# Batched x·y on one core: loading each block of x two batches earlier and splitting its transposes into halves

## The chip, the cores and the metric

One core of one Trainium2 chip. The metric is device time in microseconds (us), the median of the runs given. All runs quoted are fast (on one core: within 1.5% of the fastest of the same kernel) unless the text says otherwise. A profiled run has a span about 1.8 us shorter than its device time (134.7 us against 136.52 for the kernel before), because the span counts from the program's first instruction to its last.

In the profile PE is the matrix engine (PEld its weight loads); ACT, DVE and POOL work on elements; SP issues the transfers, and SPq is its queue. HBM is the memory outside the core, SBUF the core's own, and PSUM the one that PE writes its results to. The granted clock is the share of PE's full speed that the throttle allowed. A DMA share adds up the recorded times of all packets and divides by sixteen engines' time; it can exceed 1, so the records must overlap a little.

## The reference

```python
batch, dim_i, dim_j, dim_k = 32, 256, 512, 384     # x: b,i,j   y: b,j,k   float32
def reference(x, y):
    return np.einsum('bij,bjk->bik', x, y).astype(np.float32)
```

That is 32 independent products of 256 x 512 by 512 x 384. x is 16.8 MB, y 25.2 MB and the result 12.6 MB, so 54.5 MB cross between HBM and SBUF.

## The kernel before

x is loaded in blocks of Q = 4 batches (2048 KB in one transfer), y batch by batch (768 KB), and results are stored batch by batch (384 KB). The products need x transposed. PE does that in 32 transposes per block into PSUM; ACT and DVE copy the transposed tiles out as fp16 ("evictions", eight of 128x512 per block). ACT and DVE also round y to fp16 and copy the products out of PSUM ("collect"). All transfers are issued from one queue, SP, in program order.

```python
def load(b):
    if b % Q == 0:                       # x of batches b..b+3, just before y of b
        x_of[b // Q] = x_pool.tile([P, R, J], F32, name="x_sb")
        keep(nc.sync.dma_start(out=x_of[b // Q], in_=x[b : b + Q]...))
    y_of[b] = y_pool.tile([P, NJ, K], F32, name="y_sb")
    keep(nc.sync.dma_start(out=y_of[b], in_=y[b]...))

def transpose(q):                        # a whole block: 4 x 2 tiles
    for t in range(NJ):
        for e in range(NI):
            ...                          # 4 PE transposes into t_ps
            if n % 2 == 0: keep(nc.vector.tensor_copy(dst, t_ps))
            else:          keep(nc.scalar.copy(dst, t_ps))
# ... cut: round_y, multiply, collect, store ...

ahead = LAG - 2                          # LAG = 8: loads run six batches ahead
for b in range(ahead): load(b)
for s in range(B + 2):
    if s + ahead < B:          load(s + ahead)
    if s >= 2:                 collect(s - 2)
    if 1 <= s <= B:            multiply(s - 1)
    if s < B and s % Q == 0:   transpose(s // Q)
    if s < B:                  round_y(s)
    if s >= 2:                 store(s - 2)
```

Buffers that matter: 3 of x, 10 of y, 2 of transposed x, 10 of results, 4 PSUM banks for transposes and 4 for products.

Of the kernel before, what the change touches and what calls it, by code (L numbers as in the profile page):

```python
# [1 line left out]

# [5 lines left out]


MM_DT = mybir.dt.float16  # L10
F32 = mybir.dt.float32
P = 128


Q = 4

LAG = 8

ON_ACT = ()


@with_exitstack
def kernel(
    ctx: ExitStack,
    tc: tile.TileContext,
    x: bass.AP,
    y: bass.AP,
    out: bass.AP,
):
    nc = tc.nc  # L30

    B, I, J = x.shape
    _, _, K = y.shape

    NI = I // P
    NJ = J // P


    R = Q * NI
    PQ = P // Q  # L40

    const_pool = ctx.enter_context(tc.tile_pool(name="const", bufs=1))
    x_pool = ctx.enter_context(tc.tile_pool(name="x_pool", bufs=3))
    y_pool = ctx.enter_context(tc.tile_pool(name="y_pool", bufs=10))
    yr_pool = ctx.enter_context(tc.tile_pool(name="yr_pool", bufs=4))
    xt_pool = ctx.enter_context(tc.tile_pool(name="xt_pool", bufs=2))
    o_pool = ctx.enter_context(tc.tile_pool(name="o_pool", bufs=10))
    tpsum_pool = ctx.enter_context(tc.tile_pool(name="tpsum", bufs=4, space=bass.MemoryType.PSUM))
    opsum_pool = ctx.enter_context(tc.tile_pool(name="opsum", bufs=4, space=bass.MemoryType.PSUM))


    keep = tc.keep_in_program_order

    identity = const_pool.tile([P, P], F32)
    make_identity(nc, identity)

    x_of, y_of, yr_of, xt_of, ps_of, o_of = {}, {}, {}, {}, {}, {}

    def load(b):
        if b % Q == 0:  # L60
            x_of[b // Q] = x_pool.tile([P, R, J], F32, name="x_sb")
            keep(
                nc.sync.dma_start(  # L63
                    out=x_of[b // Q],
                    in_=x[b : b + Q].rearrange("g (p r) j -> (g p) r j", r=R),
                )
            )
        y_of[b] = y_pool.tile([P, NJ, K], F32, name="y_sb")
        keep(nc.sync.dma_start(out=y_of[b], in_=y[b].rearrange("(q t) k -> q t k", q=P)))  # L69

    def transpose(q):




        x_sb = x_of.pop(q)
        xt_of[q] = xt_pool.tile([P, Q, NJ, NI, PQ, Q], MM_DT, name="xt_sb")
        n = 0
        for t in range(NJ):
            for e in range(NI):  # L80
                t_ps = tpsum_pool.tile([P, Q, Q, PQ], F32, name="t_ps")
                for h in range(Q):
                    keep(
                        nc.tensor.transpose(  # L84
                            t_ps[:, h].rearrange("c g p -> c (g p)"),
                            x_sb[:, h * NI + e, t::NJ],
                            identity,
                        )
                    )
                dst = xt_of[q][:, :, t, e].rearrange("c g p h -> c h g p")  # L90
                if n % 2 == 0:
                    keep(nc.vector.tensor_copy(dst, t_ps))  # L92
                else:
                    keep(nc.scalar.copy(dst, t_ps))  # L94
                n += 1

    def round_y(b):
        y_sb = y_of.pop(b)
        yr_of[b] = yr_pool.tile([P, NJ, K], MM_DT, name="y_r")
        for t in range(NJ):  # L100
            if t % 2 == 0:
                keep(nc.scalar.copy(yr_of[b][:, t], y_sb[:, t]))  # L102
            else:
                keep(nc.vector.tensor_copy(yr_of[b][:, t], y_sb[:, t]))  # L104

    def multiply(b):
        xt_sb, y_r = xt_of[b // Q][:, b % Q], yr_of.pop(b)
        ps_of[b] = [
            opsum_pool.tile([P, K], F32, name=f"o_ps_{e}", tag="o_ps")
            for e in range(NI)  # L110
        ]
        for t in range(NJ):
            for e in range(NI):
                keep(
                    nc.tensor.matmul(  # L115
                        ps_of[b][e],
                        xt_sb[:, t, e].rearrange("c p h -> c (p h)"),
                        y_r[:, t],
                        start=(t == 0),
                        stop=(t == NJ - 1),  # L120
                    )
                )

    def collect(b):
        o_of[b] = o_pool.tile([P, NI, K], F32, name="o_sb")
        for e in range(NI):
            if e % 2 == 0:
                keep(nc.scalar.copy(o_of[b][:, e], ps_of[b][e]))  # L128
            else:
                keep(nc.vector.tensor_copy(o_of[b][:, e], ps_of[b][e]))  # L130
        del ps_of[b]

    def store(b):
        eng = nc.scalar if b in ON_ACT else nc.sync
        keep(eng.dma_start(out=out[b].rearrange("(m e) k -> m e k", m=P), in_=o_of.pop(b)))


    ahead = LAG - 2
    for b in range(ahead):
        load(b)  # L140
    for s in range(B + 2):
        if s + ahead < B:
            load(s + ahead)
        if s >= 2:
            collect(s - 2)
        if 1 <= s <= B:
            multiply(s - 1)
        if s < B and s % Q == 0:
            transpose(s // Q)
        if s < B:  # L150
            round_y(s)
        if s >= 2:
            store(s - 2)


# [1 line left out]
_INS = ['x', 'y']  # L157
_OUTS = [((32, 256, 384), 'float32')]


# [23 lines left out]
```

## Time and profile before

| | before |
|---|---|
| device time, median of 3 (range) | 136.25 us (136.09 to 136.34) |
| span of the profiled run | 134.7 us |
| busy PE / ACT / DVE | 89.5 / 80.1 / 73.7 us |
| 16 DMA engines busy with data | 97.9% of the span |
| mean rate over the span | 405 GB/s |

How to read it: start with the rows that can be full. No compute engine is; the DMA engines are. Then ask whether an average hides a stage with another limit. One view is who made the compute engines wait; the columns are total us, number of waits, longest.

```profile
ACT xt_sb L94 <- PE t_ps L84: 43.9, 16, 8.7
DVE xt_sb L92 <- PE t_ps L84: 40.2, 18, 9.8
...
PE t_ps L84 <- DMA x_sb<-in_x_dram: 24.3, 7, 8.7
```

These are the waits that the change is aimed at. ACT and DVE stood for some 40 us each in front of an eviction. Laid over PE's own waits, ACT's 43.9 us are 22.3 us in which PE stood before a transpose whose x had not landed (6.7 of them at the start) and 21.6 us in which PE was at work; DVE's 40.2 us are 24.3 and 15.9.

### The profile page before, as it was taken

To read this page: it belongs to the slowest core of one execution; us is meant where nothing else is said; L and a number is where in the kernel's file an instruction comes from. 1 tells how busy PE (TensorE), PEld (TensorE's weight loads), DVE (VectorE), ACT (ScalarE), POOL (GpSimd) and SP (SyncE) were. 2 spreads that over 40 slices of the span, in tenths; PEclk is the share of its full clock that TensorE was granted. 3 is DMA by queue.
4 is the path that set the end of the run, shared out by engine and by line. 5 is a ranking of instruction groups with operands and counts; after the bars stand their busy time and mean duration, and the time that the engine had idled before them with its cause. 6 is when DMAs were issued, how large, how long until landed. Compare 5 with 4: busy or idle time off the path is not lost.

```text
span 134.7 us, 1539 instructions
## 1 busy us (share of the span) xinstructions
PE 89.5 (66%) x512; PEld 66.6 (49%) x512; DVE 73.7 (55%) x128; ACT 80.1 (59%) x129; POOL 0.7 (1%) x6
## 2 busy tenths in 40 slices
PE   0049499769677908949794983949459492794920
PEld 0048368644564408925492543936259360793510
DVE  0008855975397503873489340796228870378720
ACT  3007994996299602795479650699218990179910
POOL 2000000000000000000000000000000000000000
PEclk9999999999999985686999599599995999559995
DMA  5999999999999999999999999999999999999992
GB/s 131 399 413 423 447 412 416 416 434 414 404 422 451 425 399 424 421 435 437 400 416 430 438 425 410 421 418 454 407 409 425 433 440 402 421 421 413 412 410 84
DMA packets 10375, 54.62 MB, mean 405 GB/s; under 512 B 1152, under 2 KB 1152, under 8 KB 9344
## 3 DMA queue, kind: packets, MB, share of 16 engines
q1 hardware_dynamic: 10368, 54.53, 97.9%
q8 instruction: 4, 0.07, 0.2%
q14 instruction: 3, 0.02, 0.0%
HBM read 41.94 MB, written 12.58 MB: 405 GB/s over the span
## 4 chain that ended last, share of the span: by engine, by line
DMA 79%; PE 8%; ACT 5%; DVE 2%; issue 2%; SPq 1%; DVEq 0%
DMA y_sb<-in_y_dram 30%; DMA x_sb<-in_x_dram 27%; DMA out_dram<-o_sb 21%; PE o_ps L115 4%; PE t_ps L84 4%; ACT xt_sb L94 2%; ACT y_r L102 2%; DVE xt_sb L92 1%; DVE y_r L104 1%; DVE o_sb L130 0%; SPq L69 0%; ACT o_sb L128 0%; SPq L63 0%; DVEq L130 0%
## 5 line engine op out<-in xcount | busy, mean ns | idle before, releaser
L94 ACT CAST xt_sb<-t_ps 128x512 f16<-128x512 f32 x32 | 39.8, 1350 | 44.0 <-PE t_ps L84 43.9
L92 DVE CAST xt_sb<-t_ps 128x512 f16<-128x512 f32 x32 | 40.1, 1323 | 40.3 <-PE t_ps L84 40.2
L84 PE MATMUL t_ps<-identity,x_sb 128*128 128x128 f32 x256 | 43.4, 340 | 24.5 <-DMA x_sb<-in_x_dram 24.3
L115 PE MATMUL o_ps<-y_r,xt_sb 128*128 128x384 f16 x256 | 46.3, 342 | 14.9 <-ACT y_r L102 14.9
L84 PEld LDWEIGHTS t_ps<-identity,x_sb 128*128 128x128 f32 x256 | 41.1, 216 | 27.8 <-issue 26.4
L115 PEld LDWEIGHTS <-xt_sb 128*128 128x128 f16 x256 | 26.2, 102 | 34.2 <-issue 19.9
L102 ACT CAST y_r<-y_sb 128x384 f16<-128x384 f32 x64 | 30.2, 527 | 0.6 <-DMA y_sb<-in_y_dram 0.6
L130 DVE COPY o_sb<-o_ps 128x384 f32<-128x384 f32 x32 | 17.8, 556 | 15.1 <-PE o_ps L115 15.1
L104 DVE CAST y_r<-y_sb 128x384 f16<-128x384 f32 x64 | 19.9, 354 | 0.4 <-DMA y_sb<-in_y_dram 0.4
L128 ACT COPY o_sb<-o_ps 128x384 f32<-128x384 f32 x32 | 15.4, 483 | 3.8 <-PE o_ps L115 3.8
L94 ACT ACT_TABLE_LOAD x1 | 1.3, 1283 | 0.7 <-PEq L168 0.7
masks.py:199 POOL TENSOR_SCALAR_AFFINE_SELECT identity<-identity 128x128 f32<-128x128 f32 x1 | 0.3, 294 | 0.1
masks.py:197 POOL MEMSET identity<- 128x128 f32 x1 | 0.2, 205 | 0.3 <-POOLq L168 0.3
L168 POOL MEMSET const-bfloat16-1.0<- 128x1 bf16 x1 | 0.1, 102 | 0.0
L168 POOL MEMSET const-uint8-127<- 128x1 uint8 x1 | 0.1, 102 | 0.0
L168 POOL MEMSET const-float32-0.0<- 128x1 f32 x1 | 0.1, 99 | 0.2 <-issue 0.2
L168 POOL MEMSET const-float32-1.0<- 128x1 f32 x1 | 0.1, 99 | 0.0
## 6 DMA issues: line engine op xcount, KB each, us to landing
y_sb<-in_y_dram SPq DMA_DIRECT2D x32, 768.0 KB, 15.1
x_sb<-in_x_dram SPq DMA_DIRECT2D x8, 2048.0 KB, 14.2
out_dram<-o_sb SPq DMA_DIRECT2D x32, 384.0 KB, 14.1
```

What stands on the lines that cost most here:

```text
L84: nc.tensor.transpose(t_ps[:, h].rearrange("c g p -> c (g p)"), x_sb[:, h * NI + e, t::NJ], identity,)
L92: keep(nc.vector.tensor_copy(dst, t_ps))
L94: keep(nc.scalar.copy(dst, t_ps))
L102: keep(nc.scalar.copy(yr_of[b][:, t], y_sb[:, t]))
L104: keep(nc.vector.tensor_copy(yr_of[b][:, t], y_sb[:, t]))
L115: nc.tensor.matmul(ps_of[b][e], xt_sb[:, t, e].rearrange("c p h -> c (p h)"), y_r[:, t], start=(t == 0), stop=(t == NJ - 1),)
L128: keep(nc.scalar.copy(o_of[b][:, e], ps_of[b][e]))
L130: keep(nc.vector.tensor_copy(o_of[b][:, e], ps_of[b][e]))
L168: nc = _bacc.Bacc("TRN2", target_bir_lowering=False, num_devices=1)
```

## The change

The intent: each block of x is loaded two batches earlier, and its 32 transposes no longer stand as one block between the products of two batches. They follow the products of the two preceding steps in halves of 16, so that products, stores and transposes mix.

```diff
+    def load_x(q): ...                  # the same transfer as before
     def load(b):
-        if b % Q == 0: ...              # x block of b
+        if b == 0:
+            load_x(0)
+        if b % Q == Q - 2 and b + 2 < B:
+            load_x((b + 2) // Q)
         ...
-    def transpose(q):
+    def transpose(q, half):
-        for t in range(NJ):
+        for t in range(half * NJ // 2, (half + 1) * NJ // 2):
 ...
+        if s == 0:
+            transpose(0, 0)
+            transpose(0, 1)
         if s >= 2:
             collect(s - 2)
         if 1 <= s <= B:
             multiply(s - 1)
-        if s < B and s % Q == 0:
-            transpose(s // Q)
         if s < B:
             round_y(s)
+        for half in range(2):
+            if s % Q == Q - 2 + half and s + 2 < B:
+                transpose(s // Q + 1, half)
```

More of the change, by code (lines that the diff above doesn't have):

```diff
@@ L57, with load_x @@
     x_of, y_of, yr_of, xt_of, ps_of, o_of = {}, {}, {}, {}, {}, {}
-    def load(b):
-        if b % Q == 0:
-            x_of[b // Q] = x_pool.tile([P, R, J], F32, name="x_sb")
-            keep(
-                nc.sync.dma_start(
-                    out=x_of[b // Q],
-                    in_=x[b : b + Q].rearrange("g (p r) j -> (g p) r j", r=R),
-                )
-            )
+    def load_x(q):
+        x_of[q] = x_pool.tile([P, R, J], F32, name="x_sb")
+        keep(
+            nc.sync.dma_start(
+                out=x_of[q],
+                in_=x[q * Q : (q + 1) * Q].rearrange("g (p r) j -> (g p) r j", r=R),
+            )
+        )
+    def load(b):
+        if b == 0:
+            load_x(0)
+        if b % Q == Q - 2 and b + 2 < B:
+            load_x((b + 2) // Q)
         y_of[b] = y_pool.tile([P, NJ, K], F32, name="y_sb")
         keep(nc.sync.dma_start(out=y_of[b], in_=y[b].rearrange("(q t) k -> q t k", q=P)))
-    def transpose(q):
-        x_sb = x_of.pop(q)
-        xt_of[q] = xt_pool.tile([P, Q, NJ, NI, PQ, Q], MM_DT, name="xt_sb")
+    def transpose(q, half):
+        x_sb = x_of[q]
+        if half == 0:
+            xt_of[q] = xt_pool.tile([P, Q, NJ, NI, PQ, Q], MM_DT, name="xt_sb")
         n = 0
-        for t in range(NJ):
+        for t in range(half * NJ // 2, (half + 1) * NJ // 2):
             for e in range(NI):
```

## The prediction

> **What bounds the kernel now.** I read the page first: busy shares, the 40 slices, the DMA queue line.
>
> ```profile
> PE 89.5 (66%) x512; PEld 66.6 (49%) x512; DVE 73.7 (55%) x128; ACT 80.1 (59%) x129; POOL 0.7 (1%) x6
> ...
> DMA  5999999999999999999999999999999999999992
> ...
> q1 hardware_dynamic: 10368, 54.53, 97.9%
> ...
> HBM read 41.94 MB, written 12.58 MB: 405 GB/s over the span
> ```
>
> No compute engine is above 66%, while the one data queue fills 97.9% of sixteen DMA engines' span, and every slice but the first and the last is full. The kernel is a copy with arithmetic beside it.
>
> Then the chain of waits, to see whether that average hides a stage with another limit.
>
> ```profile
> DMA 79%; PE 8%; ACT 5%; DVE 2%; issue 2%; SPq 1%; DVEq 0%
> ```
>
> The 8% of PE and 5% of ACT could be taken for the price of the transposes. So I asked for DMA share and rate by stage (columns: stretch, length, busy time of the engines, granted clock, DMA share, GB/s).
>
> ```profile
> 3.00:18.65 15.65, 7.87 (x46) 6.69 (x47) 6.78 (x10) 7.43 (x11) 0.00 (x0) 1.00 1.00 421
> 18.65:110.30 91.65, 68.00 (x395) 49.65 (x394) 56.19 (x101) 60.22 (x101) 0.00 (x0) 0.89 1.02 423
> 110.30:123.00 12.70, 8.31 (x43) 7.27 (x42) 6.21 (x8) 5.68 (x7) 0.00 (x0) 0.73 0.99 412
> 123.00:131.00 8.00, 5.36 (x32) 3.03 (x31) 4.53 (x12) 5.50 (x14) 0.00 (x0) 1.00 1.02 412
> ```
>
> The share stays at 0.99 to 1.02 in the loads before the first store, in the steady part, in the stretch with the last block of transposes (PE's clock down to 0.73), and in the stores at the end. The rate moves by 3%. No stage has another limit.
>
> Last, the waits of the queue that issues every transfer, and the end of its timeline.
>
> ```profile
> SPq L135 <- DMA x_sb<-in_x_dram: 28.7, 6, 6.0
> SPq L135 <- DMA y_sb<-in_y_dram: 26.6, 18, 1.5
> SPq L69 <- DMA out_dram<-o_sb: 11.3, 20, 0.6
> SPq L135 <- DVE o_sb L130: 11.2, 6, 4.0
> ```
>
> ```profile
> 110.31 0.33 SPq L69 DMA_DIRECT2D y_sb<-in_y_dram  x1
> 115.23 14.73 SPq L135 DMA_DIRECT2D out_dram<-o_sb  x9
> ```
>
> A store at L135 doesn't read x, yet it waits for an x transfer. Numbering the 72 transfers in order of issue, from the ninth on each leaves only when the one eight places before it has landed: y6 at 8.58 us, when x0 had landed at 8.56; y7 at 10.44 after y0 at 10.43; x2 at 12.34 after y1 at 12.32. So eight are in flight, and a wait for a transfer means that the queue is full. The fourth line is another thing: six stores waited 11.2 us in all for compute, 4.0 us at most, with seven transfers under way (store 23, at 115.23, is the start of the last nine).
>
> **What the Trainium skill says.** "DMA: Bandwidth & Descriptors", section "Where 436 GB/s comes from", puts the ceiling of the sixteen SBUF ports at 435 GB/s and a measured 16 MB load at 425. The trace agrees: 421 to 423 while the queue is full, so there is no rate to win. The same page, section "Why a DMA increments its semaphore by 16 and not by 1", says that up to sixteen engines work on one transfer and finish independently, and that only the full count means landed. The trace's landing records show it: the ten transfers that landed first (28.5 us and before) had 0.8 us between their first and last engine; all later ones have 2.1 to 2.5 us. "TensorE: Matmul & The Clock Gate", section "What's actually happening", says that an idle PE drops to half clock. The trace shows grants of 0.5 after each long wait for x. The change may help here, but PE doesn't set the end.
>
> **The change part by part.**
>
> 1. Loads of x moved ahead by two batches. Removed: nothing; added: nothing. It stays 8 x loads of 2048 KB, 32 y loads of 768 KB and 32 stores of 384 KB. From the packet records one engine's share is 64 packets of 16 KB at 0.611 us, 256 of 6 KB at 0.234 and 256 of 3 KB at 0.121: 39.1 + 59.9 + 31.0 = 130.0 us. The slowest engine began at 1.74 and ended at 133.58, 131.84 us. The other 1.8 us are slow first packets (1.0 to 2.1 us each) and one 16 KB instruction fetch of 1.1 us at 28.4, beside which an x packet took 1.08 instead of 0.61. The slowest engine has thus no idle time to give back. Effect: 0.
>
> 2. Transposes in two halves. Still 256 transposes and 64 evictions of the same shapes. A half is 16 transposes (32 took 4.54 us at full clock, so 2.3) and two evictions on each of ACT and DVE, 2 x 1.35 = 2.7 us. On ACT a step with a half costs 2.7, plus two roundings 2 x 0.527 and a collection 0.483: 4.2 us; a step without one 1.5. Batches arrive every (768 + 384) KB at 421 GB/s, 2.8 us, and a block of x takes 5.0 us more: 4 x 2.8 + 5.0 = 16.2 us per four batches, against 16.1 between the x issues at 52.83 and 68.89. ACT needs 2 x 4.2 + 2 x 1.5 = 11.4 of those. Two steps with halves fall 2 x 1.4 = 2.8 us behind, and the next two win 2.6 back, before the pause of 5.0 for the next x. PE waits for x (24.3 us over 7 in the groups of instructions) should shrink or move to waits for y. This is all beside the DMA.
>
> 3. Could stores become late enough to hurt? A transfer takes 14.1 (stores) to 15.1 us (y) from issue to landing at the median, nearly all of it queueing. A store held for 4 us leaves over 9 us of queued work; a delay of 2.8 us does so all the more. Effect in the middle: 0.
>
> 4. The start. After the change x1 goes before y2, so y2 lands at about 14.2 + 5.0 = 19.2 us rather than 14.20. Batch 0's store left at 18.65 and can leave only when the transfer eight before it, now y2, has landed, 0.5 us later, with seven loads queued. Effect: 0.
>
> 5. The end. y31's load is issued after store 22 and before store 23 in both programs, so the same transfers stand before it and the same nine stores after it. On the slowest engine y31 landed at 125.40; nine stores of 8 packets x 0.121 = 0.97 (landings lie 0.94 apart) give 125.40 + 9 x 0.94 = 133.9, and the last store did land at 133.91. Compute is earlier after the change: y31 rounded 1.0 us after landing, multiplied in 1.3, collected in 0.56, so the last store is ready near 128.4 instead of 129.63. But it then waits in the queue. The faster engines get about 0.2 us closer together; the slowest ends no earlier. Effect: 0, at most -0.2.
>
> Sum: 136.25 + 0 - 0.05 = 136.2 us.
>
> **Rivals.** (a) The end was set by compute: the last store is issued within 0.1 us of the last eviction, and it lands 4.3 us later, the shortest of all stores. If the queue were dry there, 1.2 us would be won: 135.0. Against it: the arithmetic of part 5, and landings that keep their 0.94 us spacing up to the last. (b) The transposes stall the store queue and the DMA runs dry in every group; 4.0 us of waiting in each of 7 groups would promise up to 11 us, so 125. Against it: the share of 1.02 in 18.65 to 110.30, and the 2.3 us between first and last engine, which stays from 34.9 us to the end and would shrink if all engines drained. (c) The halves delay roundings until the eight in flight run out, some 2.8 us in one or more groups: 139. Against it: the 9 us of queued work. (d) The instruction fetches (16 KB each, at 28.4, 58.1, 89.9 and 121.3) fall on other DMA engines, or two on one. Each costs its engine about 1.5 us, so the end could move from 0.7 us earlier to 1.5 later. The trace tells nothing against it, and it sets the width of my range.
>
> **Range and chances.** The centre is 136.2. The repeats spread over 0.25 us; (d) and a small part of (a) widen it to 135.3 to 137.0. Over 2% is 2.7 us: that needs (b) or (c), 1% each. Within 2%: 98%.
>
> **What would show it right or wrong.** Right: the data queue at 97 to 98% again, DMA share near 1.0 in every stretch between 3 and 131 us, landings of the last nine stores 0.94 us apart, while the waits of evictions for transposes and of PE for x fall, the stores' waits for compute fall, and the last store leaves near 128.4 us. Wrong: a stretch in mid-kernel with the share clearly under 1, a rate away from 421, or a last store that lands much less than nine spacings after y31. If the time moves by over 1 us with the share unchanged, the packet time or the spread of the engines moved, which I did not foresee.

## The result

| | before | after |
|---|---|---|
| device time, median of 6 (range) | 136.26 us (136.09 to 136.47) | 136.32 us (136.06 to 136.55) |
| ratio | | 1.0002 (95%: 0.9988 to 1.0016) |

A ratio here is the mean time of one kernel's fast runs over that of the other's fast runs of the same rounds, so it is not quite the ratio of the medians.

The page of the changed kernel, the same rows as the prediction showed:

```profile
PE 86.9 (64%) x512; PEld 64.0 (47%) x512; DVE 71.1 (53%) x128; ACT 78.4 (58%) x129; POOL 0.7 (1%) x6
...
DMA  4999999999999999999999999999999999999992
...
q1 hardware_dynamic: 10368, 54.53, 97.9%
```

Its chain of waits by engine:

```profile
DMA 88%; DVE 3%; ACT 2%; PE 1%; SPq 1%; issue 0%; DVEq 0%; ACTq 0%
```

Stretches (columns: stretch, length, busy time of PE, weight loads, DVE, ACT and POOL, granted clock, DMA share, GB/s):

```profile
3.00:18.65 15.65, 8.10 (x39) 6.86 (x40) 6.05 (x8) 6.62 (x8) 0.00 (x0) 0.94 0.98 415
18.65:110.30 91.65, 65.73 (x397) 48.05 (x396) 53.50 (x97) 57.82 (x97) 0.00 (x0) 0.91 1.02 422
110.30:123.00 12.70, 10.13 (x63) 7.65 (x62) 9.16 (x18) 9.93 (x17) 0.00 (x0) 0.91 1.02 420
123.00:131.00 8.00, 2.92 (x16) 1.45 (x15) 2.44 (x7) 2.75 (x7) 0.00 (x0) 0.91 1.02 412
```

Waits of the compute engines:

```profile
DVE y_r L110 <- DMA y_sb<-in_y_dram: 37.7, 11, 6.5
ACT y_r L108 <- DMA y_sb<-in_y_dram: 35.0, 8, 6.4
...
PE t_ps L90 <- DMA x_sb<-in_x_dram: 25.8, 6, 8.7
...
DVE xt_sb L98 <- PE t_ps L90: 12.4, 5, 9.8
ACT xt_sb L100 <- PE t_ps L90: 11.6, 5, 8.6
```

Waits of the issuing queue for compute, and its last nine stores:

```profile
SPq L141 <- DVE o_sb L136: 9.7, 5, 3.2
```

```profile
115.27 13.27 SPq L141 DMA_DIRECT2D out_dram<-o_sb  x9
```

What to see. The compute side did change. The waits for transposes fell from 43.9 and 40.2 us to 11.6 and 12.4; in the last 8 us of stores PE is busy 2.92 us where it was 5.36, because the products are already done; the chain has 1% of PE in it instead of 8%. And the queue's line is the same to the digit, while the DMA share of each stretch stays within 0.03 of what it was. The waits that vanished in front of the evictions came back in front of the roundings of y, 35.0 and 37.7 us, as waits for a DMA. With the data queue full all the time, removing one wait of a compute engine only lets it reach the next transfer sooner.

The landing records of the trace say where the end comes from (first and last of the sixteen DMA engines, us from the start):

```
                    before             after
y31 landed          123.04 / 125.40    123.21 / 125.42
store 31 issued     129.63             128.21
store 31 landed     131.79 / 133.91    131.74 / 133.95
```

The last store left 1.42 us earlier and landed at the same time.

### The profile page after: what moved, and what is told of

It is laid out like the page before. It is cut to its first block, busy times and chain, and to the rows that moved or that the text cites. A ratio compares the mean times of both kernels' runs of the same rounds, so it can differ in the third digit from the quotient of the medians.

```text
span 134.8 us, 1531 instructions
## 1 busy us (share of the span) xinstructions
PE 86.9 (64%) x512; PEld 64.0 (47%) x512; DVE 71.1 (53%) x128; ACT 78.4 (58%) x129; POOL 0.7 (1%) x6
## 3 DMA queue, kind: packets, MB, share of 16 engines
q1 hardware_dynamic: 10368, 54.53, 97.9%
## 4 chain that ended last, share of the span: by engine, by line
DMA 88%; DVE 3%; ACT 2%; PE 1%; SPq 1%; issue 0%; DVEq 0%; ACTq 0%
DMA y_sb<-in_y_dram 67%; DMA out_dram<-o_sb 21%; DVE xt_sb L98 2%; PE o_ps L121 1%; ACT y_r L108 1%; ACT xt_sb L100 1%; DVE y_r L110 0%; ACT o_sb L134 0%; DVE o_sb L136 0%; SPq L74 0%; SPq L62 0%; DVEq L110 0%; ACTq L108 0%; SPq L141 0%
## 5 line engine op out<-in xcount | busy, mean ns | idle before, releaser
L121 PE MATMUL o_ps<-y_r,xt_sb 128*128 128x384 f16 x256 | 49.1, 341 | 14.4 <-ACT y_r L108 14.4
L90 PE MATMUL t_ps<-identity,x_sb 128*128 128x128 f32 x256 | 41.4, 326 | 26.2 <-DMA x_sb<-in_x_dram 25.8
L90 PEld LDWEIGHTS t_ps<-identity,x_sb 128*128 128x128 f32 x256 | 38.9, 214 | 29.5 <-issue 27.6
L108 ACT CAST y_r<-y_sb 128x384 f16<-128x384 f32 x64 | 29.7, 516 | 35.5 <-DMA y_sb<-in_y_dram 35.0
L100 ACT CAST xt_sb<-t_ps 128x512 f16<-128x512 f32 x32 | 39.4, 1354 | 11.6 <-PE t_ps L90 11.6
L98 DVE CAST xt_sb<-t_ps 128x512 f16<-128x512 f32 x32 | 39.5, 1330 | 12.4 <-PE t_ps L90 12.4
L110 DVE CAST y_r<-y_sb 128x384 f16<-128x384 f32 x64 | 19.8, 354 | 38.4 <-DMA y_sb<-in_y_dram 37.7
L136 DVE COPY o_sb<-o_ps 128x384 f32<-128x384 f32 x32 | 18.3, 570 | 6.1 <-PE o_ps L121 6.1
L134 ACT COPY o_sb<-o_ps 128x384 f32<-128x384 f32 x32 | 16.8, 525 | 1.7 <-PE o_ps L121 1.7
```

The costliest lines, as they stand in the source:

```text
L90: nc.tensor.transpose(t_ps[:, h].rearrange("c g p -> c (g p)"), x_sb[:, h * NI + e, t::NJ], identity,)
L108: keep(nc.scalar.copy(yr_of[b][:, t], y_sb[:, t]))
L110: keep(nc.vector.tensor_copy(yr_of[b][:, t], y_sb[:, t]))
L121: nc.tensor.matmul(ps_of[b][e], xt_sb[:, t, e].rearrange("c p h -> c (p h)"), y_r[:, t], start=(t == 0), stop=(t == NJ - 1),)
L134: keep(nc.scalar.copy(o_of[b][:, e], ps_of[b][e]))
L136: keep(nc.vector.tensor_copy(o_of[b][:, e], ps_of[b][e]))
```

## The experiments

The theory: the transfers keep the slowest DMA engine busy from its first packet to its last, so no rearrangement of compute moves the end. (The trace does not name the engine of a packet; that one engine is the slowest all along is inferred from the even spacing of the last landings.) The rivals: the end is set by compute; stores held up by transposes drain the queue; the two parts of the change cancel each other. Twelve kernels were run. Ratios are to the kernel before unless said otherwise.

### stores_free: no store waits for arithmetic

```diff
+    fixed = const_pool.tile([P, NI, K], F32, name="fixed")
+    nc.gpsimd.memset(fixed, 0.0)
-        ... in_=o_of.pop(b)
+        ... in_=fixed
```

> Edit: every store reads one constant tile that is filled once, so no store waits for arithmetic; all loads, transposes, products and evictions stay (wrong result on purpose). My theory (the 16 DMA engines have no idle time, the slowest ends 9 stores after y31): 136.2 us, within 0.4 of before, data queue at 97 to 98%. Rival 'the end is set by compute' : about 135.0 us, 1.2 less. Rival 'stores held by the transposes drain the queue in each group': 125 to 133 us.

Measured: 136.33 us, ratio 1.0003 (0.9991 to 1.0016). Its output is wrong, which doesn't matter for the time. The last store was issued at 126.17 us, 3.5 us before that of the kernel before, and landed at 133.72. With every wait of a store for compute gone, the time is the same, so the late stores cost nothing. This rules out the first two rivals for the real kernel.

### copy_only: the 72 transfers alone

```diff
+    (stores read the constant tile, as above; the identity for the transposes goes too)
-        if s >= 2: collect(s - 2)
-        if 1 <= s <= B: multiply(s - 1)
-        if s < B and s % Q == 0: transpose(s // Q)
-        if s < B: round_y(s)
```

> Edit: all arithmetic taken away, the 72 transfers stay in their order, stores read a constant tile (wrong result on purpose). My theory: 134.5 to 135.4 us: the same 130 us of packets per engine, and only the 16 KB instruction fetches (about 1.5 us on the slowest engine) go, with the spread between first and last landing down from 2.3 to about 0.8 us. If the fetches cost nothing: 136.2. Rival 'compute sets a part of the time': under 133.5 us.

Measured: 135.55 us (135.50 to 135.63), ratio 0.9944 (0.9932 to 0.9956). Its data queue:

```profile
q1 hardware_dynamic: 10368, 54.53, 98.5%
```

The figure missed my range by 0.15 us at the upper end. The range was built from the landings, and there the step held: the last landing came at 132.52 us instead of 133.91, 1.4 us earlier, and the spread between first and last engine stayed at 0.73 to 0.85 us throughout instead of jumping to 2.3. But the program then took 1.3 us to end after that landing, where the kernel before takes 0.8. I had not counted that. The main result stands: taking away all arithmetic is worth 0.76 us, 0.56%. No order of the arithmetic can win more while these transfers stay as they are and in this order.

### x_early_alone and halves_alone: the two parts one by one

```diff
 x_early_alone: the changed kernel, with
-        for half in range(2):
-            if s % Q == Q - 2 + half and s + 2 < B: transpose(s // Q + 1, half)
+        if s < B and s % Q == 0:        # after multiply, as before
+            transpose(s // Q, 0)
+            transpose(s // Q, 1)
 halves_alone: the changed kernel, with
-        if b == 0: load_x(0)
-        if b % Q == Q - 2 and b + 2 < B: load_x((b + 2) // Q)
+        if b % Q == 0: load_x(b // Q)
```

> Edit: the changed kernel's loads (x two batches ahead of its y), with the transposes whole and at their old place. My theory: 136.2 us, within 0.4 of before. Rival 'two parts of the change cancel' : the early load gains or loses by itself, at least 0.8 us either way, and the halves alone do the opposite.

> Edit: the changed kernel's transposes in halves two steps ahead, with the loads of x at their old place, so that PE waits in mid-step for an x that has not landed. My theory: 136.2 us, within 0.4 of before: PE and the evictions wait longer in the profile, but a store is issued only when the transfer eight places before it has landed, some 11 us after that x, and arithmetic needs about 6. Rival 'late stores drain the queue': 1 to 3 us per group of four batches, 140 us or more.

Measured: x_early_alone 136.19 us, ratio 0.9989 (0.9978 to 1.0001); halves_alone 136.36 us, ratio 1.0001 (0.9987 to 1.0014). The parts do not cancel; each is worth nothing. halves_alone is the harder test, because PE now asks for x four steps after its load instead of six. Its waits of the queue and of PE:

```profile
SPq L139 <- DVE o_sb L134: 26.6, 14, 5.3
```

```profile
PE t_ps L88 <- DMA x_sb<-in_x_dram: 31.4, 7, 8.7
```

Stores waited 26.6 us for compute, 14 times, where they waited 11.2 us before, and the time is still equal. At the end the last store was issued at 130.74 us, 1.1 us later than before, and the sixteen engines' landings of it lay 0.7 us apart instead of 2.1: the faster engines did run dry there. The slowest one landed its last stores 0.93 to 0.99 us apart to the end (133.59) and so lost next to nothing. That is what "the slowest engine sets the end" means, and how thin the cover was. An estimate: a store with nothing before it lands 2.3 us after its issue (the last stores of the two runs with few stores, below), so this one could have landed at 133.0, and some 0.5 us more of lateness would have shown. The same sum gives 2.0 us for the kernel before.

### before_few_stores and after_few_stores: uncover the end

```diff
-        if s >= 2:
+        if s >= 2 and (s - 2) % 16 == 15:
             store(s - 2)
```

> Edit to the kernel before: only the stores of batches 15 and 31 remain (wrong result on purpose), so the nine stores behind the last load no longer cover the end. The packets per engine fall from 130 to about 101 us. My theory: the last load lands near 103 us, x7 near 96, and the last block of transposes (6.6 us), four products and a store follow: 112 to 115 us. If compute cannot keep up with a DMA period of 12.4 us per four batches, more.

> The same edit to the changed kernel. My theory: the work behind the last load shrinks to one batch, so 1.5 to 3 us less than the same edit of the kernel before: 110 to 112.5 us. This would show that the change does shorten the work after the last load, and that in the real kernel nine queued stores hide it. Rival 'the rearrangement is worth nothing to the compute side': equal within 0.5 us.

Measured: 115.39 us and 114.63 us, ratios 0.8465 and 0.8409, so the changed kernel is 0.7% or about 0.8 us faster than the one before under this edit (0.8409 / 0.8465 = 0.993). Their outputs are wrong, which doesn't matter for the times. The direction held, the sizes did not: before was 0.4 us over its range, after 2.1 us over, and the gap was half of the least I had expected. The trace of after tells why. With few stores a y lands every 1.9 us, but a step with a half takes about 3.3, so the two steps with x7's halves ended late. The roundings of y28 started at 102.6 us though it had landed at 99.7, and four products (5.4 us from 103.58) instead of one stood behind the last load, just as in the kernel before (5.4 us from 105.04). In the two profiled runs those four products start 1.5 us earlier, which is the whole difference between these runs (116.15 and 114.70 us). But the profiled run of before is the slowest of its five, at a granted clock of 0.947 where the others have 0.967 to 0.999, so the 0.8 us of the medians is the better figure for what the change wins at this end.

### before_lag4 and after_lag4: a shorter lead

```diff
-LAG = 8
+LAG = 4
```

> Edit to the kernel before: the loads run two batches ahead rather than six. Then a block of transposes (5.3 to 6.6 us), the roundings and the collection stand between the landing of x and the next store, with only 5 to 6.5 us of transfers behind it. My theory: the queue drains by 1 to 2 us in each group: 140 to 150 us. If the lead of six is not what hides the transposes: 136.2.

> The same edit to the changed kernel. My theory: a half block (2.7 to 3.3 us) fits into the 5 to 6.5 us, so the queue stays nearly full: 136 to 140 us, at least 2 us less than the same edit of the kernel before. Rival 'the rearrangement is worth nothing': equal to the kernel before with two batches ahead.

Measured: fast runs of 146.89 and 148.85 us, ratio 1.0847 (1.0788 to 1.0905), and of 146.09 and 146.10, ratio 1.0716 (1.0698 to 1.0735). Two runs of each were over 1.5% above the fastest of their kernel and are left out, though the runs spread so evenly (146.09 to 150.91 us) that this may be the kernels' own spread; with two fast runs apiece, the difference between the kernels (1.0716 / 1.0847, so 1.2%) is thinly supported. The kernel before did as expected. The changed one did not: I expected 136 to 140. Waits of its queue, and one stretch in mid-kernel (the last two numbers are DMA share and GB/s):

```profile
SPq L141 <- DVE o_sb L136: 98.8, 25, 14.3
```

```profile
40.00:120.00 80.00, 50.73 (x285) 37.12 (x283) 40.40 (x73) 43.97 (x74) 0.00 (x0) 0.83 1.00 392
```

Nearly every store now waits for compute, and a share of 1.00 goes with 392 GB/s instead of 422. The engines are "busy", but with longer packets: data packets of 16 KB take 0.667 us in the mean instead of 0.626, 6 KB packets 0.253 instead of 0.235, 3 KB packets 0.1224 instead of 0.1212. For one engine that is 64 x 0.041 + 256 x 0.018 + 256 x 0.0012 = 7.5 us of the 9.8 lost. My step failed where it took a queue that is not empty for one that loses nothing. The loss does not come while the queue is short: from 35 to 45 us, with the transfers in flight down to four, the rate was 430 GB/s, and from 45 to 55 us, when it had been refilled to eight, 376. The long packets stand just after such refills, as they do in the first microseconds of every run (1 to 2 us for most of the first 16 KB packets). Why they are long is open; no run here separates the cause.

### before_lag6 and after_lag6: between the two

```diff
-LAG = 8
+LAG = 6
```

> Edit to the kernel before: the loads run four batches ahead rather than six. With a lead of two the loss was about 11 us over eight blocks of x, 1.4 us each; two more batches are 5.6 us more of transfers behind each wait. My theory (a wait costs time only when it outlasts what is queued): the loss is gone, 136.3 us within 0.5. Rival 'the loss shrinks with the lead in proportion': about 142.

> The same edit to the changed kernel: 136.3 us within 0.5 by my theory, equal to the same edit of the kernel before; about 141 by the rival.

Measured: 136.22 us, ratio 0.9993 (0.9979 to 1.0008), and 136.26 us, ratio 0.9998 (0.9982 to 1.0015). A lead of four batches is enough for both kernels. The loss does not shrink in proportion to the lead; it is gone once the waits fit into what is queued. So the lead of six had two batches of slack already, and the two more that the change gives to x had nothing left to hide.

### before_evict_twice and after_evict_twice: make compute the bound

```diff
-                if n % 2 == 0: keep(nc.vector.tensor_copy(dst, t_ps))
-                else:          keep(nc.scalar.copy(dst, t_ps))
+                for again in range(2):
+                    if n % 2 == 0: keep(nc.vector.tensor_copy(dst, t_ps))
+                    else:          keep(nc.scalar.copy(dst, t_ps))
```

> Edit to the kernel before: each transpose block is copied out of PSUM twice (result unchanged), so ACT gets 15.4 us of work per four batches and DVE 14.5, against 16.1 of DMA. In mid-kernel a store has about 16 us after its x lands, so it still fits. At the end the last block lands at 115.2, its evictions take 10.6 instead of 5.3 us, and the last store is ready near 133 instead of 129.6, later than the queue reaches it. My theory: 137 to 141 us, all of the loss at the end. Rival 'the transposes cost the queue time in each group': 8 x 5.3 us more, up to 178.

> The same edit to the changed kernel. x7 lands about 5.6 us earlier and is transposed before y28 is needed. My theory: 136 to 139 us, 1 to 3 us less than the same edit of the kernel before: the change is worth something once arithmetic sets the end. Rival 'the change is worth nothing': equal.

Measured: 166.04 us, ratio 1.218 (1.2151 to 1.221), and 154.75 us, ratio 1.1352 (1.13 to 1.1404). The results are correct. Both are far above what I expected, and the change is worth 6.8% here (1.1352 / 1.218 = 0.932). The timeline of the kernel before with this edit:

```profile
85.64 10.09 DVE L93 CAST xt_sb<-t_ps 128x512 f16<-128x512 f32 x8 [1.21 <-PE t_ps L84]
86.13 10.08 ACT L95 CAST xt_sb<-t_ps 128x512 f16<-128x512 f32 x8 [1.94 <-PE t_ps L84]
...
96.58 1.76 PE L116 MATMUL o_ps<-y_r,xt_sb 128*128 128x384 f16 x5 [4.06 <-ACT y_r L103]
```

and of the changed kernel with it:

```profile
78.86 5.15 DVE L99 CAST xt_sb<-t_ps 128x512 f16<-128x512 f32 x4 [0.87 <-PE t_ps L90]
79.35 5.14 ACT L101 CAST xt_sb<-t_ps 128x512 f16<-128x512 f32 x4 [1.47 <-PE t_ps L90]
...
80.12 1.47 PE L122 MATMUL o_ps<-y_r,xt_sb 128*128 128x384 f16 x8
```

In the first, all evictions of a block run as one piece of 10.1 us, no y can be rounded meanwhile, and PE stands 4.06 us before the next product; then products run while ACT and DVE have gaps. In the second the piece is half as long and a product runs under it. The time from one issue of x to the next, from the issue times of the traces, is 19.0 us ((117.13 - 60.18) / 3) against 17.3 ((102.46 - 50.64) / 3); 1.7 us times seven blocks is 12, and 11.3 were measured. My expectation had added up 15.4 us of ACT work per block and compared it with 16.1 us of DMA, as if a queue of in-order engines that wait for one another could be filled to 96%. They cannot: a serial stretch of evictions plus a serial stretch of products is longer than either engine's busy time. This is the very thing that the change shortens. Which of its two parts earns the 6.8% was not tried.

## Why the prediction was right

- **The bound.** Right. DMA share 0.98 to 1.02 in all four stretches after as before, queue at 97.9% in both, and 0.56% to be had by removing all arithmetic.
- **Part 1, 0 for moving the loads.** Right by x_early_alone (0.9989).
- **Part 2, 0 for the halves.** Right by halves_alone (1.0001) for the time. Its working rested on sums of busy time per engine, which the doubled evictions show to be too kind to a chain of in-order engines; at the real load there was room enough to hide that error.
- **Part 3, late stores do not hurt.** Right by stores_free and halves_alone. But two steps of its reason fail. "Seven transfers under way" holds for one of the six waits, the 4.0 us of store 0; the other five stood before the last five stores, which left with five or four transfers under way, so that the cover of the last store was about 2 us and not 9. And "over 9 us of queued work" treats any queue that is not empty as full rate, which the runs with a shorter lead refute.
- **Part 4, the start.** y2 landed at 19.04 us (19.2 predicted). The first store left at 19.89, 1.2 us later than before rather than 0.5. It waited for arithmetic and not for y2: DVE finished its collection at 19.81, since the products before it took 4.44 us for 16 matmuls, at a granted clock of 0.50 from 18 to 20 us. Without effect, as said.
- **Part 5, the end.** Right nearly to the digit: y31 at 125.42 (125.40 before), last store issued at 128.21 (128.4 predicted), landed at 133.95 (133.9 predicted). The faster engines did not get closer, as they should have by 0.2 us: the last store's landings lay 2.12 us apart before and 2.21 after.
- **Signs to look for.** The waits of evictions fell as predicted. PE's wait for x did not (24.3 us before, 25.8 after): the transposes moved forward by as many steps as the loads. In x_early_alone, where they stay at their old place, PE's wait for x is 9.0 us, one wait at the start. The stores' wait for compute fell only from 11.2 to 9.7 us.
- **Rivals.** (a) fell with stores_free and part 5, though the cover was only about 2.0 us, and 0.5 in halves_alone. (b) fell with stores_free; its 4.0 us in each group was a misreading too, since that wait was store 0's and no other wait of a store for compute before 116 us was over 1.4 us. (c) did not occur in the changed kernel. (d), the instruction fetches, moved to 28.2, 54.4, 86.7 and 118.4 us, the spread at the end is 2.1 and 2.2 us, and the end did not move.
- **The clock.** "Grants of 0.5 after each long wait for x" is too simple a reading of the kernel before: it holds for the four waits of 2.7 to 3.9 us, but the clock was 1.00 after the first and longest (8.7 us), and 0.50 also from 60 to 63 and from 74 to 76 us, at waits of 1.9 us for a rounded y. Nothing rested on it.

The Trainium skill's page "Runtime: NRT & Kernel Launch", section "Instruction fetch mechanics", says that instructions are refilled in 16 KiB blocks of 256 by a DMA queue of the sequencer's own. The trace agrees: four packets of 16 KB on a separate instruction queue in the kernels with PE work, none in copy_only. That copy_only alone keeps a spread of 0.8 us, and that the jump to 2.3 us in the kernel before falls at its first fetch (28.4 us), makes the fetch the likely cause of those 1.4 us. The other traces agree: in all thirteen with PE work the first fetch falls somewhere between 24.9 and 36.5 us, the spread is 0.5 to 1.1 us up to it and 1.7 to 2.4 us at the first or second landing after it. As no run takes the fetch alone away, it isn't shown in isolation.

## What to carry to other kernels

When the transfers fill every stretch, a shorter compute chain is worth nothing however many waits it removes; run the transfers alone first, and the difference (here 0.56%) is all that reordering the arithmetic beside them can win. The same rearrangement was worth 6.8% once evictions set the pace, so keep it in mind for kernels whose serial stretches of evictions and products add up to more than the transfers. Judge queues by the rate as well as by the share of busy time: a share of 1.02 went with 422 GB/s in one kernel, and one of 1.00 with only 392 in another.

## What the Trainium skill lacked or had wrong

- "DMA: Bandwidth & Descriptors" describes queues and a first-byte latency, but not that packets grow longer just after a shrunken queue is refilled: 6 KB packets took 0.253 us in the mean with a lead of two batches and 0.235 with six, at a busy share of 1.00 and 1.02, and the rate fell from 422 to 392 GB/s.
- "Runtime: NRT & Kernel Launch" tells of the 16 KiB instruction blocks, but gives no figure for what a fetch may cost transfers that fill the DMA engines: the packet records show 1.1 us for the fetch at 28.4 us and 1.08 instead of 0.61 us for an x packet right after it.
